# Trunk kernel, end of the last feed-forward layer: other chunk sizes, and the last 384 tokens multiplied with the weights moving

## The chip, the cores and the metric

The kernel runs on one core of one Trainium2 chip. The metric is the device time of one execution in microseconds (us): the median of the runs, 2497.24 us before the change (three runs, 2496.61 to 2497.68). One further execution was recorded by the profiler, and all views below are of that one.

The engines are named as in the profile: PE is the matrix engine (PEld its loads of the stationary operand), DVE the vector engine, ACT the scalar engine, POOL the GpSimd engine, SP the engine that issues most transfers.

## What is computed

Two layers over 640 tokens (512 of a new stream, 8 times 16 of running streams) of width 1024. A layer is a half-step feed-forward, a mixer (short convolution and chunk-band attention), and a second half-step feed-forward. A final normalization ends it:

```python
def _rmsnorm(x, g):
    xf = x.astype(jnp.float32)
    y = xf * lax.rsqrt(jnp.mean(xf * xf, axis=-1, keepdims=True) + EPS)
    return y.astype(x.dtype) * g

def _swiglu(h, w_gu, w_down):
    gu = h @ w_gu
    g, u = jnp.split(gu, 2, axis=-1)
    return (jax.nn.silu(g) * u) @ w_down
...
        xp = xp + 0.5 * _swiglu(_rmsnorm(xp, norm_ffn2[l]), w_ffn2_gu[l], w_ffn2_down[l])
...
    y_prompt = _rmsnorm(xp, norm_final)
    y_sample = _rmsnorm(xs, norm_final)
```

The hidden width of the feed-forward is 2816, which is 22 tiles of 128; the width 1024 is 8 tiles of 128. Everything is float32.

## The kernel before

**Layout.** The residual stream `x` lies in SBUF as eight tiles `x[0]` to `x[7]`, features on the 128 partitions and the 640 tokens along them. Every float32 product is made of three products of a faster format: an operand is split into a rounded part `hi` (ACT casts it, line 340 for weights, tile `whi`) and the rest `lo` (DVE subtracts, line 345, tile `wlo`), and `hi*hi`, `hi*lo` and `lo*hi` are added up in PSUM. Weights come as slabs of 128x1024 in the order of use, loaded by SP (tile `raw`, 512 KB each), and at most three split slabs exist at once (`bufs=3`).

**The four feed-forwards** are a0, b0 (layer 0) and a1, b1 (layer 1). The order of each is laid out by `ffn_order` from a list of chunk sizes, `FFNS`. Within a chunk the gate and up products of each of its hidden tiles are made (`gate_up`, one hidden tile j at a time), and the down products of the chunk before are spread between them.

- `gate_up` multiplies a 2x2 arrangement of blocks with seven block products in place of eight (the Strassen-Winograd scheme). Each block product is twelve matmuls of 320 columns: tiles `pa`, `pb`, `pc` in PSUM, line 435. The sums of weight blocks that it needs are made by DVE on the slabs (line 282); for the slabs that `LEAN` names, one of these sums is made by POOL instead, with two transfers of which the second adds to the first (`lend`, lines 267 and 268, tile `lent`).
- A chunk of four tiles that does not reach the end (`by_seven`) has its down products made the same way, in two units of seven block products each (`down_rows`, tiles `da`, `db`, `dc`, line 1110). Their results go into `x` partly by DVE (line 1137), partly through SBUF (`c1`, `c5`, `u2`) and a POOL transfer that adds in place (line 1132).
- Any other chunk has its down products made plainly (`product`, tile `pd`, line 411).

b1 has the chunks 3, 4, 4, 4, 4, 3: the first is done plainly, four by seven, and the last is handed to `Final`. In the stream this reads: gate-up of tiles 0 to 2, then tile 3 to 6 with a plain piece of the first chunk's down product behind each, and so on; at the end gate-up 19 and 20, a `down_rows` unit, gate-up 21, a `down_rows` unit, and the end. a1 and a0 have the chunks 4, 4, 4, 4, 4, 2; b0 has 4, 4, 4, 4, 6.

**The end, `Final`** (lines 1884 to 1969), works in the layout of `x`, features on the partitions. The tokens fall into two parts, 384 and 256 (`PARTS`). For each part and each of the eight feature tiles m, `product` makes nine matmuls (three hidden tiles, three products each; tile `pdf`, line 1938) with a block of weights stationary and the tokens moving; `take` adds half of that to `x[m]` (DVE, line 1943), squares it (ACT, line 1945) and adds the squares up over m (DVE, line 282, tile `fsum`). When a part is through, the sum over the features, which lies across partitions, is made by narrow matmuls against ones (tile `npsf`, line 519); ACT takes the root (line 1956), DVE the reciprocal (line 1961), a product with `fold` (line 529) and two matmuls (tile `nbcf`, line 538) spread the result over the partitions again, and `out` scales each `x[m]` by it and by the gain (DVE, line 1967) and sends it off (line 1969, SP and ACT queues). For the second part all of this follows the last matmul.

**Order.** PE, DVE and ACT run in the order in which the program is written here (`tc.manual_schedule`); for the middle of a feed-forward, from tile `free` on, only PE does. SP and POOL take their instructions as the planner places them. PSUM has eight banks of 512 float32 a partition; `layout` deals them out, in b1 four as two `acc` tiles and four as `att`.

Of the kernel before, what the change touches and what calls it, by code (L numbers as in the profile page):

```python
# [10 lines left out]
F32 = mybir.dt.float32  # L11
# [35 lines left out]
        "a1": ((4, 4, 4, 4, 4, 2), 0), "b1": ((3, 4, 4, 4, 4, 3), 0)}  # L47

PARTS = slice(0, 3 * P), slice(3 * P, T)
# [10 lines left out]
LEAN = {"a0": (1, 6), "b0": (1, 5), "a1": (1, 5)}  # L60
# [27 lines left out]
def ffn_order(name):  # L88


    chunks, plain = FFNS[name]
    out, held, j0 = [], [], 0
    for n in chunks:
        ms = list(range(KT)) if held else []
        step = max(2, -(-KT // n))
        for j in range(j0, j0 + n):
            out.append(("std" if j < plain else "gu", j))
            if ms and by_seven(name, held[0]):
                for _ in range((ROWS if n > 2 else (1, 1)).count(j - j0)):
# [6 lines left out]
        j0 += n  # L106

    return out + [("cut", None)] + [("down", [(m, held)]) for m in range(KT)]
# [24 lines left out]
def stages():  # L133
# [10 lines left out]
    def ffn(name):  # L144
        held = 0
        for what, a in ffn_order(name):
            if what == "gu":
                plain(held)
                held = 0
                out.append("gu")  # L150
            elif what == "std":
                held += 2 * KT
            elif what == "cut":
                plain(held)
                held = 0
            elif what == "rows":
                plain(held)
                held = 0
                out.append("gu")
            else:  # L160
                held += sum(len(js) for _, js in a)
        plain(held)
# [28 lines left out]
def trunk(ctx: ExitStack, tc: tile.TileContext, xin, wst, small, pbias, samplebias, kcache, vcache,  # L191
          yout, ko, vo, co):
# [654 lines left out]
    def gate_up(fp, n, ex, first, tails, put, j, pair, later, at):  # L847
# [122 lines left out]
        def tail(weights=True):  # L970
# [206 lines left out]
    def ffn(name, fp, ex, goff, after, end=False):  # L1177
# [57 lines left out]
        for what, a in ffn_order(name):  # L1235
# [6 lines left out]
            if what == "gu":  # L1242
# [11 lines left out]
                gate_up(fp, f"{name}_{a}", ex, a == plain, tails, act.__setitem__, a, pair, later,  # L1254
                        a - chunk_at(name, a)[0])
# [5 lines left out]
            js = a[0][1]  # L1261
# [622 lines left out]
    class Final:  # L1884


        def __init__(self):
            self.st = Stats("f")
            self.ssum = [pool[0].tile([P, c.stop - c.start], F32, tag=t, name=f"fsum{a}", bufs=1)
                         for a, (c, t) in enumerate(zip(PARTS, ("ssum", "rho")))]  # L1890

        def all(self, ops):
            ws = [[tiles.take() for _ in ops] for m in range(KT)]
            flush()
            rr = pool[0].tile([P, T], F32, tag="cap", name="frr", bufs=6)[:, PARTS[0]]
            A, B = PARTS

            for m in range(KT):
                self.product(0, m, ops, ws[m])
                self.take(0, m, m < KT - 1)  # L1900
            ends = self.ssum[0], self.sq
            for m in range(KT):
                self.product(1, m, ops, ws[m])
                if m == 1:
                    self.ps = att("npsf0")[:, : A.stop // P]
                    for b in range(A.stop // P):
                        self.st.column(self.ps[:, b : b + 1], ends, b)
                    self.root(0)
                if m == 4:
                    self.st.spread([att(f"nbcf0_{i}")[:, : A.stop // 2] for i in range(2)], self.ssum[0], rr)  # L1910
                if m == 5:
                    self.ps = acc("npsf1")[:, :, 0]
                    self.add(self.ssum[1], True)
                if m > 4:
                    self.add(self.sq)
                self.take(1, m, m < 4)
                if m == 2:
                    self.turn(0)
                for k in {5: (0,), 6: (1, 2)}.get(m, ()):
                    self.out(k, A, rr)  # L1920
            self.add(self.sq, False, True)
            self.root(1)
            for k in range(3, 6):
                self.out(k, A, rr)
            self.turn(1)
            for k in range(6, KT):
                self.out(k, A, rr)
            ps = acc("nbcf1")[:, :, : (B.stop - B.start) // 2]
            self.st.rows([ps[:, i] for i in range(2)], self.ssum[1])
            for k in range(KT):  # L1930
                self.out(k, B, ps)

        def product(self, a, m, ops, ws):
            n = PARTS[a].stop - PARTS[a].start
            self.pd = att(f"pdf{a}_{m}")[:, :n]
            for k, ((xh, xl), (wh, wl)) in enumerate(zip(ops, ws)):
                for j, (w, z) in enumerate(((wh, xh), (wh, xl), (wl, xh))):
                    PE.matmul(self.pd, w, z[:, PARTS[a]], start=k == 0 and j == 0,
                              stop=k == len(ops) - 1 and j == 2)

        def take(self, a, m, added):
            xm = x[m][:, PARTS[a]]
            DVE.scalar_tensor_tensor(out=xm, in0=self.pd, scalar=0.5, in1=xm, op0=ALU.mult, op1=ALU.add)
            self.sq = self.ssum[a] if m == 0 else tmp(f"sqf{a}_{m}")[:, : xm.shape[1]]
            ACT.activation(self.sq, xm, AF.Square)
            if m and added:
                add(self.ssum[a], self.ssum[a], self.sq)

        def add(self, z, start=False, stop=False):

            for b in range(2):
                self.st.column(self.ps[:, b : b + 1], [z], b, start, stop)

        def root(self, a):
            cs = slice(PARTS[a].start // P, PARTS[a].stop // P)
            ACT.activation(self.st.s[:, cs], self.ps, AF.Sqrt,
                           bias=epst[:, 0:1], scale=1.0 / D)

        def turn(self, a):
            cs = slice(PARTS[a].start // P, PARTS[a].stop // P)  # L1960
            DVE.reciprocal(self.st.r[:, cs], self.st.s[:, cs])
            self.st.turn(self.ssum[a], self.st.r[:, cs])

        def out(self, k, c, rr):
            z = x[k][:, c]
            y = z if c == PARTS[0] else halves(z)
            DVE.scalar_tensor_tensor(out=y, in0=y, scalar=sm[:, O_GF + k : O_GF + k + 1],
                                     in1=rr, op0=ALU.mult, op1=ALU.mult)
            (ACT if c == PARTS[1] and k % 2 else SP).dma_start(yout[:, k, c], x[k][:, c])
# [34 lines left out]
def _stream(i):  # L2004
# [9 lines left out]
    for l in range(L):  # L2014
        def ffn(name, gu, down):
# [3 lines left out]
            for what, a in ffn_order(name):  # L2019
# [11 lines left out]
                elif what == "rows":  # L2031
# [5 lines left out]
                                         for o in range(2) for m in ms[r::2]]))  # L2037
                else:
# [25 lines left out]
def _layout(inputs):  # L2064
# [21 lines left out]
    return {"xin": xin, "wst": _stream(i), "small": small, "pbias": pbias, "samplebias": sbias, "kcache": kc, "vcache": vc}  # L2086
# [3 lines left out]
    "yout": (P, KT, T),  # L2090
# [38 lines left out]
```

## Time and profile before

| what | us |
| --- | --- |
| median of three runs | 2497.24 |
| lowest, highest | 2496.61, 2497.68 |
| the profiled execution, its own time | 2496.82 |
| its span, first to last instruction | 2495.0 |
| busy PE, DVE, ACT, POOL in it | 2476.9, 2136.4, 1343.9, 281.9 |

The span and what lies around it differ by 1.82 us. Times in the views count from the start of the span. In the **chain of waits** a row is the start, the length and the work of one piece of the chain that ended last, with the number of instructions merged in it; its times for PE are those of the matmuls' ends. In the **timeline** a row is the start, the duration, engine, line, operation, output and inputs, shape and number of instructions; matmuls overlap, so their pace is read from start to start and not from the duration. In the **windows** a row is a stretch of time, its length, and the busy time of PE, PEld, DVE, ACT and POOL with the number of instructions, then the granted PE clock, the share of the DMA engines and GB/s. In the **groups** a row is line, engine, operation, tiles, shape and count, then busy us and mean ns of one, then the engine's idle time before them and what ended it.

### The profile page before, as it was taken

Reading aid. Unit: us, or ns where it says so; the run is one execution under the profiler, and the core shown is the slowest. Engines: PE = TensorE matmul, PEld = TensorE weight load, DVE = VectorE, ACT = ScalarE, POOL = GpSimd, SP = SyncE. Lnnn points to the kernel's source line nnn. Section 1 sums busy time; section 2 is a strip of 40 time slices with the busy share of each in tenths; the row PEclk is TensorE's granted clock in tenths of the full one; section 3 lists DMA queues with packets and bytes.
Section 4 is the critical chain, followed back from the end, with each engine's and each line's share of the span. In section 5 each row is a group of like instructions: output and inputs, shape, how many; then the busy total and the mean of one; then the engine's idle time right before and its main releaser. Section 6 shows DMA issues by size and latency. Waiting matters only on the chain.

```text
span 2495.0 us, 44032 instructions
## 1 busy us (share of the span) xinstructions
PE 2476.9 (99%) x17424; PEld 2426.2 (97%) x17424; DVE 2136.4 (86%) x3510; ACT 1343.9 (54%) x2122; POOL 281.9 (11%) x429
## 2 busy tenths in 40 slices
PE   8999999999999999999999999999999999999998
PEld 8999999889999999999999999998899999999998
DVE  7999998888777899998799999998886778899997
ACT  6555556665444555555665555566644455455553
POOL 0211112211000001011001111122110000011111
PEclk9999999999999999999999999999999999999999
DMA  4443444335223234445334443453342232243433
GB/s 154 127 118 100 123 117 127 108 111 168 77 89 109 90 101 109 108 117 121 98 102 111 108 116 106 104 127 119 120 157 85 77 98 81 85 110 108 123 102 101
DMA packets 107087, 275.18 MB, mean 110 GB/s; under 512 B 12128, under 2 KB 50656, under 8 KB 106880
## 3 DMA queue, kind: packets, MB, share of 16 engines
q1 hardware_dynamic: 69120, 219.71, 27.6%
q0 software_dynamic: 36896, 52.01, 11.2%
q8 instruction: 136, 2.23, 0.4%
q10 hardware_dynamic: 864, 0.65, 0.1%
q14 instruction: 71, 0.58, 0.1%
HBM read 228.47 MB, written 7.94 MB: 95 GB/s over the span
## 4 chain that ended last, share of the span: by engine, by line
PE 92%; DVE 4%; ACT 2%; issue 1%; DMA 1%; SPq 0%; DVEq 0%; ACTq 0%; POOLq 0%
PE pab L435 12%; PE paa L435 11%; PE pcb L435 6%; PE daa L1110 6%; PE pca L435 5%; PE dab L1110 4%; PE py L411 4%; PE po L411 4%; PE qa L435 4%; PE pbb L435 3%; PE dca L1110 3%; PE pba L435 3%; PE ma_cv L435 2%; PE ma_qk L435 2%; PE pv L1597 2%; PE dcb L1110 2%
## 5 line engine op out<-in xcount | busy, mean ns | idle before, releaser
L340 ACT CAST whi<-raw 128x1024 fp32r<-128x1024 f32 (+2 forms) x568 | 505.8, 894 | 389.7 <-PE pba L435 41.8
L345 DVE TENSOR_TENSOR wlo<-raw,whi 128x1024 fp32r<-128x1024 f32 (+2 forms) x568 | 580.3, 1024 | 153.9 <-ACT whi L340 150.6
L340 ACT CAST whi<-s 128x1024 fp32r<-128x1024 f32 (+1 forms) x156 | 148.6, 953 | 289.5 <-issue 107.9
L435 PE MATMUL pab<-xhib,whi 128*128 128x320 f32 x704 | 217.9, 309 | 0.0
L435 PE MATMUL pab<-xlob,whi 128*128 128x320 f32 x704 | 217.4, 309 | 0.0
L435 PE MATMUL pab<-xhib,wlo 128*128 128x320 f32 x704 | 217.3, 309 | 0.0
L435 PE MATMUL paa<-xloa,whi 128*128 128x320 f32 x640 | 197.7, 309 | 0.6 <-DVE xloa L672 0.6
L435 PE MATMUL paa<-xhia,whi 128*128 128x320 f32 x640 | 198.0, 309 | 0.2 <-DVE ga L282 0.2
L435 PE MATMUL paa<-xhia,wlo 128*128 128x320 f32 x640 | 197.7, 309 | 0.0
L345 DVE TENSOR_TENSOR wlo<-s,whi 128x1024 fp32r<-128x1024 f32 (+1 forms) x156 | 170.9, 1095 | 4.4 <-ACT whi L340 4.4
L1132 POOL DMA_DIRECT2D x<-c_b x64 | 56.6, 1026 | 841.9 <-DVE x L1137 502.4
L1132 POOL DMA_DIRECT2D x<-c_a x80 | 71.0, 1044 | 573.6 <-ACT ahia L1014 205.4
L435 PEld LDWEIGHTS pab<-xhib,whi 128*128 128x128 f32 x704 | 132.1, 188 | 1.1 <-issue 0.9
L435 PEld LDWEIGHTS pab<-xlob,whi 128*128 128x128 f32 x704 | 132.1, 188 | 0.0
L435 PEld LDWEIGHTS pab<-xhib,wlo 128*128 128x128 f32 x704 | 132.1, 188 | 0.0
L435 PEld LDWEIGHTS paa<-xhia,whi 128*128 128x128 f32 x640 | 120.1, 188 | 1.3 <-DVE ga L282 0.5
L435 PEld LDWEIGHTS paa<-xloa,whi 128*128 128x128 f32 x640 | 120.1, 188 | 1.1 <-DVE xloa L672 1.1
L435 PEld LDWEIGHTS paa<-xhia,wlo 128*128 128x128 f32 x640 | 120.1, 188 | 0.2
L435 PE MATMUL pcb<-xhib,wlo 128*128 128x320 f32 x352 | 108.9, 309 | 0.0
L435 PE MATMUL pcb<-xhib,whi 128*128 128x320 f32 x352 | 108.7, 309 | 0.0
L435 PE MATMUL pcb<-xlob,whi 128*128 128x320 f32 x352 | 108.7, 309 | 0.0
L282 DVE TENSOR_TENSOR raw<-s,raw 128x512 f32<-128x512 f32 x156 | 106.4, 682 | 0.0
(741 smaller groups left out, 8046.7 us busy)
## 6 DMA issues: line engine op xcount, KB each, us to landing
raw<-in_wst SPq DMA_DIRECT2D x376, 512.0 KB, 3.5
x<-c_a POOLq DMA_DIRECT2D x80, 160.0 KB, 4.4
x<-c_b POOLq DMA_DIRECT2D x64, 160.0 KB, 3.8
kc<-in_kcache SPq DMA_DIRECT2D x32, 256.0 KB, 4.7
vc<-in_vcache SPq DMA_DIRECT2D x16, 512.0 KB, 4.4
lent<-in_wst POOLq DMA_DIRECT2D x26, 256.0 KB, 4.0
x<-u_a POOLq DMA_DIRECT2D x40, 160.0 KB, 4.0
x<-u_b POOLq DMA_DIRECT2D x32, 160.0 KB, 4.2
```

Source lines behind the costliest of these rows:

```text
L282: DVE.tensor_tensor(out=out, in0=a, in1=b, op=op)
L340: ACT.copy(hi[:, d], src[:, c])
L345: DVE.tensor_tensor(out=lo, in0=src, in1=hi.bitcast(F32), op=ALU.subtract)
L411: PE.matmul(ps[:, a, :HT], w, x[a] if isinstance(x, tuple) else x[:, a * HT : (a + 1) * HT], start=first and j == 0 and not seeded, stop=l ...
L435: PE.matmul(ps, a, b, start=start and kp == 0 and j == 0, stop=stop and kp == NP - 1 and j == 2, skip_group_check=True)
L1110: PE.matmul(ps[u], w, y, start=start and i == 0 and j == 0, stop=i == 1 and j == 2, skip_group_check=True)
L1132: POOL.dma_start(x[ms[2 * u + r]][:, cols], z[:, u], accum_op=ALU.add)
L1597: PE.matmul(pv[t], xx[:, t * P : (t + 1) * P], w[:, kk * AW : (kk + 1) * AW], start=c == 0 and kk == 0 and j == 0, stop=c == KT // 2 - 1 a ...
```

## The change

The chunks of b1 become 4, 4, 4, 4, 4, 2 and `LEAN` gets an entry for b1. So five chunks are done by seven, the first among them, and two hidden tiles are left for the end; the last two `down_rows` units follow each other.

In the end the tokens fall into 256 (`FEAT`) and three groups of 128 (`GROUPS`). The 256 are done as before, with six matmuls a feature tile in place of nine. For each group of 128, `x` is turned by eight PE transposes into two PSUM banks (tokens on the partitions, 512 features each), and twelve matmuls add the down product to that, with the tokens' block stationary and 512 columns of weights moving. Each such half is squared by ACT with a running sum along the row; the row's sum gives the token's factor without a sum across partitions. The first half is multiplied by the gain at once (DVE) and by the factor later (ACT), the second half by both in one DVE instruction; each half goes out with a transfer of its own, one from SP and one from ACT. The gain comes as a new input of 128x1024, the same row on every partition, and these tokens leave through a new output `yrows`. The factor one half of the feed-forward is folded into the last two hidden tiles (`halve`). A root is taken of an unused value behind the first squares.

```diff
-        "a1": ((4, 4, 4, 4, 4, 2), 0), "b1": ((3, 4, 4, 4, 4, 3), 0)}
-
-PARTS = slice(0, 3 * P), slice(3 * P, T)
+        "a1": ((4, 4, 4, 4, 4, 2), 0), "b1": ((4, 4, 4, 4, 4, 2), 0)}
+
+FEAT = 2 * P
+GROUPS = (T - FEAT) // P
...
-LEAN = {"a0": (1, 6), "b0": (1, 5), "a1": (1, 5)}
+LEAN = {"a0": (1, 6), "b0": (1, 5), "a1": (1, 5), "b1": (1, 5)}
...
             else:
-                DVE.tensor_tensor(out=u, in0=u, in1=g, op=ALU.mult)
+                if halve:
+                    DVE.scalar_tensor_tensor(out=u, in0=u, scalar=0.5, in1=g, op0=ALU.mult, op1=ALU.mult)
+                else:
+                    DVE.tensor_tensor(out=u, in0=u, in1=g, op=ALU.mult)
...
+            self.ssum = pool[0].tile([P, FEAT], F32, tag="ssum", name="fsum", bufs=1)
+            self.acc = sp.tile([P, 2 * GROUPS], F32, tag="facc", name="facc", bufs=1)
+            self.root = sp.tile([P, 3 * GROUPS], F32, tag="froot", name="froot", bufs=1)
 
         def all(self, ops):
-            ws = [[tiles.take() for _ in ops] for m in range(KT)]
+            ws = [slab(hold[0])[0] for _ in ops]
             flush()
+            layout("e", 0)
+            self.g = wp.tile([P, D], F32, tag="raw", name="gfin", bufs=3)
+            SP.dma_start(self.g, gfin)
+            rr = pool[0].tile([P, T], F32, tag="cap", name="frr", bufs=6)[:, :FEAT]
+            st, nb = self.st, FEAT // P
+            self.rows = [[pr(f"prow{i}{h}") for h in range(2)] for i in range(2)]
+            self.y = [pool[0].tile([P, D], F32, tag="raw", name="yrow0", bufs=1)]
+            self.y += [wp.tile([P, D], F32, tag="raw", name=f"yrow{i}", bufs=3) for i in range(1, GROUPS)]
 
             for m in range(KT):
+                self.product(m, ops, ws)
+                self.take(m)
+                if m == 0:
+                    ACT.activation(early, self.ssum[:, 0:1], AF.Sqrt)
+            for i in range(2):
+                self.turned(i)
+            ps = att("npsf")[:, :nb]
+            for b in range(nb):
+                st.column(ps[:, b : b + 1], (self.ssum, self.sq), b)
+            ACT.activation(st.s[:, :nb], ps, AF.Sqrt, bias=epst[:, 0:1], scale=1.0 / D)
+            DVE.reciprocal(st.r[:, :nb], st.s[:, :nb])
+            st.turn(self.ssum, st.r[:, :nb])
+            self.half(0, 0, ops, ws)
+            self.half(0, 1, ops, ws)
+            st.spread([att(f"nbcf{i}")[:, : FEAT // 2] for i in range(2)], self.ssum, rr)
+            self.rows.append([att(f"prow2{h}") for h in range(2)])
+            self.turned(2)
+            for k in range(4):
+                self.out(k, rr)
+            self.half(1, 0, ops, ws)
+            for k in range(4, 6):
+                self.out(k, rr)
+            self.half(1, 1, ops, ws)
             for k in range(6, KT):
+                self.out(k, rr)
+            for h in range(2):
+                self.half(2, h, ops, ws)
+
+        def product(self, m, ops, ws):
+            self.pd = att(f"pdf{m}")[:, :FEAT]
             for k, ((xh, xl), (wh, wl)) in enumerate(zip(ops, ws)):
                 for j, (w, z) in enumerate(((wh, xh), (wh, xl), (wl, xh))):
+                    PE.matmul(self.pd, w[:, m * P : (m + 1) * P], z[:, :FEAT], start=k == 0 and j == 0,
                               stop=k == len(ops) - 1 and j == 2)
 
+        def take(self, m):
+            xm = x[m][:, :FEAT]
+            add(xm, self.pd, xm)
+            if m > 1:
+                add(self.ssum, self.ssum, self.sq)
+            self.sq = self.ssum if m == 0 else tmp(f"sqf{m}")[:, :FEAT]
             ACT.activation(self.sq, xm, AF.Square)
+
+        def turned(self, i):
+            c = slice(FEAT + i * P, FEAT + (i + 1) * P)
+            for m in range(KT):
+                h, o = divmod(m, KT // 2)
+                PE.matmul(self.rows[i][h][:, o * P : (o + 1) * P], x[m][:, c], ident, is_transpose=True,
+                          start=o == 0, stop=False, skip_group_check=True)
+
+        def half(self, i, h, ops, ws):
+            tokens = slice(FEAT + i * P, FEAT + (i + 1) * P)
+            c = slice(h * CH // 2, (h + 1) * CH // 2)
+            ps, y = self.rows[i][h], self.y[i]
+            for k, ((xh, xl), (wh, wl)) in enumerate(zip(ops, ws)):
+                for j, (z, w) in enumerate(((xh, wh), (xl, wh), (xh, wl))):
+                    PE.matmul(ps, z[:, tokens], w[:, c], start=False,
+                              stop=k == len(ops) - 1 and j == 2, skip_group_check=True)
+            s = self.acc[:, 2 * i + h :][:, 0:1]
+            part, root, r = (self.root[:, 3 * i + o :][:, 0:1] for o in range(3))
+            ACT.activation(tmp(f"sqr{i}{h}")[:, : CH // 2], ps, AF.Square, accum_out=s)
+            if h == 0:
+                DVE.tensor_tensor(out=y[:, c], in0=ps, in1=self.g[:, c], op=ALU.mult)
+                DVE.tensor_scalar(out=part, in0=s, scalar1=1.0 / D, scalar2=EPS, op0=ALU.mult, op1=ALU.add)
+                return
+            ACT.activation(root, s, AF.Sqrt, bias=part, scale=1.0 / D)
+            DVE.reciprocal(r, root)
+            DVE.scalar_tensor_tensor(out=y[:, c], in0=ps, scalar=r, in1=self.g[:, c],
+                                     op0=ALU.mult, op1=ALU.mult)
+            SP.dma_start(yrows[i][:, c], y[:, c])
+            c = slice(0, CH // 2)
+            ACT.activation(y[:, c], y[:, c], AF.Copy, scale=r)
+            ACT.dma_start(yrows[i][:, c], y[:, c])
+
+        def out(self, k, rr):
+            z = x[k][:, :FEAT]
+            DVE.scalar_tensor_tensor(out=z, in0=z, scalar=sm[:, O_GF + k : O_GF + k + 1],
                                      in1=rr, op0=ALU.mult, op1=ALU.mult)
+            SP.dma_start(yout[:, k], z)
```

`layout("e", 0)` deals the eight PSUM banks anew, four as `pr` and four as `att`.

More of the change, by code (lines that the diff above doesn't have):

```diff
@@ L159, in ffn @@
                 out.append("gu")
+            elif what == "ends":
+                held += KT * len(a)
             else:
@@ L2037, in ffn @@
                                          for o in range(2) for m in ms[r::2]]))
+                elif what == "ends":
+                    held += [d[m][j] for j in a for m in range(KT)]
                 else:
```

84 lines of the change are left out of this document (13 added, 71 removed).

## The prediction

> **What bounds the kernel now.** I read the page first, then the busy time by windows, then the chain of waits over the last feed-forward, then the timeline of each engine behind it.
>
> ```profile
> span 2495.0 us, 44032 instructions
> ...
> 2200.00:2300.00 100.00, 100.00 (x684) 100.00 (x683) 91.54 (x147) 52.33 (x74) 16.06 (x18) 1.00 0.46 115
> 2488.00:2495.00 7.00, 0.00 (x0) 0.00 (x0) 3.51 (x9) 0.00 (x0) 0.00 (x0) 0.50 0.64 225
> ```
>
> Inside b1 PE has no gap (100 of 100 us), with DVE close behind at 91.54. So there a matmul less is time less, as long as DVE keeps up. The last 7 us are the opposite: PE does nothing, DVE scales, the transfers land.
>
> ```profile
> 2459.14 0.35 PE pdf L1938 x2
> 2459.49 1.87 PE dab L1110 x12
> 2461.36 2.80 PE pdf L1938 x16
> ...
> 2488.77 2.74 DVE x L1967 x7
> ```
>
> In the chain the last `down_rows` unit would end at 2461.36 - 0.35 = 2461.01 without the two early `pdf` matmuls. From there to the end of the span are 33.99 us: this is what the new end replaces. I call the end of that unit T0 and work out first how far T0 moves, then how long the new end is.
>
> **Part 1: the chunks.** Four plain pieces of chunk 0 go, two `down_rows` units of seven block products come.
>
> ```profile
> 835.16 1.76 PE pab L435 x12
> ...
> 910.85 1.77 PE dab L1110 x12
> ...
> 1636.80 2.00 PE dba L1110 x12
> ...
> 1647.61 14.08 PE pda L411 x96
> ...
> 2068.24 1.76 PE pab L435 x12
> ...
> 2119.48 5.28 PE pdb L411 x36
> ```
>
> Removed: 4 x 5.28 = 21.12. Added: 2 x 7 x 1.76 = 24.64. That is 3.52 more on PE (the moved hidden tile leaves the end, below). Whether DVE can feed it is read from b0, which already begins with four by seven and the same `LEAN`: from 835.16 to its first `down_rows` at 910.85 are 75.69 us for six gate-ups of 7 x 1.76 = 12.32, so 1.77 over. b1 now: 2068.24 to 2119.48, 51.24 for four, 1.96 over. So the more costly preparation on DVE, ACT and POOL is hidden behind PE's block products there, and I cost it at nothing; without that cover it is the fourth rival. Two `down_rows` units in a row stand at the end of a1: its second unit's second block took 2.00 against 1.76, and the plain product behind it began with no gap. That is 0.24 more. T0 moves by 3.76, bounds 3.5 (no such gap, b0's 0.2 gained) and 4.2 (the gap twice, 0.2 for b0's way): to 2464.77.
>
> **Part 2: PE's work in the new end**, paces read from start to start in the timeline.
>
> ```profile
> 429.80 0.39 PE L1597 MATMUL pv<-whi,hhim 128*128 128x512 f32 x1
> ...
> 433.88 0.39 PE L1597 MATMUL pv<-whi,hhim 128*128 128x512 f32 x1
> ...
> 514.73 2.34 PE L1681 MATMUL ptp<-ident,s 128*128 128x128 f32 x20
> 516.83 0.39 PE L435 MATMUL ma_qk<-thi,whi 128*128 128x320 f32 x1
> ...
> 2473.34 0.28 PE L1938 MATMUL pdf<-ahib,whi 128*128 128x256 f32 x1
> ...
> 2475.36 0.28 PE L1938 MATMUL pdf<-ahib,wlo 128*128 128x256 f32 x1
> ...
> 2479.76 0.59 PE L538 MATMUL nbcf<-fsum,ones 64*128 64x192 f32 x4 [0.19 <-DVE fsum L529]
> ...
> 2481.55 0.31 PE L519 MATMUL npsf<-ones,fsum 128*32 128x1 f32 x16
> ...
> 2482.05 0.38 PE L1938 MATMUL pdf<-ahib,whi 128*128 128x256 f32 x1
> ```
>
> 256 tokens moving: 18 matmuls, 2.02 over 17 steps, 0.119 each; 48 of them are 5.7. Weights moving, 512 columns, token block stationary, is what the `pv` product of the mixer does: 19 matmuls, 4.08 over 18 steps, 0.227; a half of six is 1.36, six halves 8.2. Transposes: 20 in 2.10, 0.105 each; 24 are 2.5. Sums for two columns with two summands: 0.50. Spread: 0.59. Together 17.5. The six halves have six banks, so PE waits for no evacuation in between.
>
> A page of the Trainium skill speaks against the transposes: "TensorE: Matmul & The Clock Gate", section "Part 4: PE-mode transpose", gives about 275 ns for one. It is a rival below.
>
> **Part 3: what PE waits for in it.** Times from here are from T0.
>
> ```profile
> 1647.96 0.88 DVE L1137 SCALAR_TENSOR_TENSOR x<-daa,x 128x320 f32<-128x320 f32 x2
> ...
> 2460.60 2.43 POOL L1132 DMA_DIRECT2D x<-u_b  x2
> ...
> 2475.52 1.28 ACT L1956 ACT_TABLE_LOAD   x1
> 2476.81 0.26 ACT L1956 ACTIVATE nrmsf<-npsf,epst 128x3 f32<-128x3 f32 x1
> ...
> 2480.49 0.42 DVE L282 TENSOR_TENSOR fsum<-fsum,sqf 128x256 f32<-128x256 f32 x1 [0.54 <-ACT sqf L1945]
> 2480.84 0.42 DVE L1943 SCALAR_TENSOR_TENSOR x<-pdf,x 128x256 f32<-128x256 f32 x1
> ```
>
> In a1 DVE was done with the unit's last results at 1647.96 + 0.88, T0 + 1.23. A step over 256 columns takes it 0.42, the next starts 0.35 later. The first square (an estimate of 0.42 from the same width on DVE) ends near 2.1; then the root that stands behind it makes ACT load its table, 1.28, and takes 0.26: the second square ends near 4.0. Moved forward to here, the load holds up the squares queued behind it on ACT, and DVE with them, because the running sum waits for the square in DVE's own queue, ahead of the next feature tile. From 4.0 DVE needs 0.42 and five more tiles of 0.70: the last sum at about 7.9, the last square with it. PE, with four `att` banks, is not held in the products (tile 3's bank is free by 4.8, product 7 starts at 5.0); it ends them at 5.7, the sixteen transposes at 7.4, and waits until 8.0: **0.6 of stall**. The bounds are 0 (table load as early as it could be) and 2.0 (a step of 0.42 + 0.42 in place of 0.70 and 0.6 of hand-offs).
>
> A rule would make more of the load: the Trainium skill, "ScalarE: Activation LUTs", section "What ACT_TABLE_LOAD costs", puts a drain of about 1380 ns beside the 1283 ns. Here the root began at 2476.81, right where 2475.52 + 1.28 ends, so the trace shows no drain behind the load. By the rule the stall would be 2.0 and the forecast 2493.0.
>
> The transposes read tokens that POOL still adds into. Its last two additions were issued from 2460.60 to 2463.03, 0.4 before the old T0 and 2.0 after it. A landing 4.0 behind an issue (the `lent` row below, also from POOL; an estimate here) is at most T0 + 4.8 for the second's start; the transposes begin at 5.7. Hidden, 0.9 to spare; each us of lateness beyond costs one. The gain's load (512 KB, SP) is needed at 10 by the first multiplication, and its buffer is given up by the slabs before T0, with SP's queue empty of weights by then: hidden by about 10 us of PE work. If not, its landing is paid.
>
> **Part 4: after the last matmul.** On PE the sums end at 8.5, two halves at 11.3, the spread at 11.9, eight transposes at 12.7, four halves at 18.2.
>
> ```profile
> 456.34 1.87 ACT L1603 ACTIVATE v<-pv,ninvm 128x512 f32<-128x512 f32 x3
> ...
> 519.31 0.72 ACT L1844 ACTIVATE yc<-yc,st 128x512 f32<-128x512 f32 x1
> 519.92 0.19 ACT L1844 ACTIVATION_READ_ACCUMULATOR yc<-yc,st 128x1 f32 x1
> ...
> L1969 ACTq DMA_DIRECT2D out_yout<-x x4: 339/344/354, 2489.2 to 2491.5; - x4
> ...
> L1687 DVE COPY pt<-ptp 128x512 f32<-128x512 f32 x22 | 14.0, 680 | 3.1 <-PE ptp L1681 3.1
> ...
> 2488.30 3.22 DVE L1967 SCALAR_TENSOR_TENSOR x<-x,sm,nbcf 128x256 f32<-128x256 f32 x8
> ```
>
> ACT does for each pair of halves two squares with a running sum (0.61 and 0.09 each until the next can start, 0.70), a root 0.26, a scaled copy of 512 columns (1.87 / 3 = 0.62), the issue of a transfer 0.34, and waits some 0.3 for DVE's reciprocal in the middle: 2.9, against 2.72 of PE. So ACT falls behind a little, and the copies of `nbcf` come on top; I put the last square at 19.5 rather than 18.9, bounds 18.9 and 20.5. Then the root 0.26, the reciprocal and its hand-off 0.2, DVE's multiplication from PSUM 0.68 (the row of that width): 20.65. Now the last DVE step ends at 2491.52 and the span 3.5 later, with 128 KB in the last transfer; here two of 256 KB leave at once. The 7 us window moved 225 GB/s, so 384 KB more is at most 1.7; I take 0.5, bounds 0 and 1.7. The new end lasts 20.65 + 3.5 + 0.5 = **24.65**.
>
> **The sum.** 2464.77 + 24.65 = 2489.4 against a span of 2495.0: **5.6 less**. The profiled execution took 2496.82, 0.42 under the median of the runs; 2496.82 - 5.6 = 2491.2 for it, and 2497.24 - 5.6 = **2491.6** for the median. Read another way: 33.99 becomes 24.65, and 3.76 of that is given back as `down_rows`. With the cheap bounds (0.3 in part 1, 0.6, 0.6, 0.5) it is 2489.6; part 3, ACT and transfers at their dear bounds (0.4, 1.4, 1.0, 1.2) give 2495.6.
>
> **The rivals.**
>
> First, *ACT and DVE pace the end.* If nothing of ACT's steps overlaps, a pair costs 2 x (0.72 + 0.19) + 0.26 + 0.62 + 0.34 + 0.3 = 3.3, 0.4 more in each of the two pairs ahead of the last square; with the stall at 2.0 and the transfers 0.5 dearer the loss is 0.8 + 1.4 + 0.5 = 2.7: 2494.3. For it: three engines hand on in strict order, and DVE's eight `out` steps stand between reciprocals. Against it: ACT's own steps do overlap in the rows of part 4 (519.31 to 519.92 is 0.61 for a step of 0.72).
>
> Second, *transposes at their full duration.* A transpose's record is about 0.27 long, and if PE could not overlap them, 24 would cost 24 x (0.27 - 0.105) = 4.0 more: 2495.6. Twenty in 2.34 speak against it; that these are added onto by later matmuls is not in any row.
>
> Third, *the change doesn't do what it says:* by seven and turned, PE's work could be no less. The window from 2488 on shows PE empty, so its old end lies up to 27 behind T0; the new one lies at 18.2, and T0 itself 3.76 later. For no gain at all some 5 us of new waits are needed, and those are the first two rivals; it gets no chance of its own.
>
> Fourth, on the other side, *the lent slabs come late at the start of b1.*
>
> ```profile
> lent<-in_wst POOLq DMA_DIRECT2D x26, 256.0 KB, 4.0
> ...
> L340 ACT CAST whi<-lent 128x512 fp32r<-128x512 f32 x13 | 8.1, 620 | 2.1 <-DMA lent<-in_wst 0.7 <-PE pab L435 0.7 <-PE paa L435 0.7
> ```
>
> b1 has none now and gets four, each two transfers of 4.0 one after the other, on POOL. From the point where the second lands after ACT wants to cast, PE waits; if it is late by one transfer, four slabs cost 4 x 4.0 = 16: 2507.6, slower. Against it: thirteen lent slabs held ACT up by 0.7 in all.
>
> **Chances.** Forecast 0.66, first rival 0.15, second 0.09, fourth 0.10. What this kernel's measurement can tell from no change is about 0.2%, 5.0 us, so "faster" ends at 2492.2, only 0.6 above the forecast. Of the forecast's 0.66 I give 0.56 to below that and 0.10 to above, as its own bounds are lopsided upwards. Faster 0.56; within 0.2% 0.10 + 0.15 + 0.09 = 0.34; slower 0.10. The range reaches from just below the sum of the cheap bounds to 2498.0, beyond the dear ones and the first two rivals together with 2 us of unknown waits; it leaves the fourth rival out. The forecast's own range is 2489.6 to 2495.6.
>
> **What would show it.** In the changed kernel's chain: T0 near 2464.8 with no new PE idle between 2068 and there (else part 1 or the fourth rival); a gap of about 0.6 on PE ahead of `npsf` (part 3); `prow` matmuls 0.227 apart and transposes 0.105 apart (part 2, second rival); the last square starting within 0.6 of its last matmul (first rival); 5.2 or less from the start of the last root to the end (0.26 + 0.2 + 0.68 + 4.0). The prediction is wrong if T0 moves by over 4.2, if PE waits inside the six halves, or if the end behind the last matmul is longer than 7.5.

## The result, and the profile after

| | before | after |
| --- | --- | --- |
| median, 12 runs each on the same chip | 2497.06 | 2491.43 |
| lowest, highest | 2496.57, 2498.21 | 2491.31, 2492.54 |
| the profiled execution, its span | 2496.82, 2495.0 | 2491.9, 2490.1 |
| T0, the end of the last `down_rows` unit | 2461.01 | 2464.56 |
| from T0 to the end of the span | 33.99 | 25.54 |

Ratio 0.9978 (95% interval 0.997 to 0.9986, which is 3.5 to 7.5 us): 5.6 us less by the medians, against 5.6 predicted. The two profiled executions differ by 4.9, because the one of after was 0.5 above its own median and the one of before 0.2 below. T0 is read as before, from the start and duration of the last block product: 2464.25 + 0.31. Each part of the forecast can be checked by these two lengths: T0 moved by 3.55 (predicted 3.76), and the new end lasts 25.54 (predicted 24.65).

First the start of b1, where the first chunk is now made by seven. From the chain of waits of the changed kernel (start, length, work), and from its windows over the same stretch (start and end, length, busy PE, PEld, DVE, ACT, POOL, granted clock, DMA share, GB/s):

```profile
2105.12 3.52 PE pab L440 x24
...
2453.74 2.02 PE dbb L1118 x12
```
```profile
2068.00:2120.00 52.00, 52.00 (x389) 50.99 (x388) 48.27 (x78) 31.77 (x51) 2.85 (x4) 1.00 0.34 102
```

The chain stays on PE, a block product every 1.76 us, and PE is busy for all of the 52 us. What the new units ask for is there, but hidden: DVE has 48.27 us of work in this window and POOL 2.85, where the kernel before has 45.43 and 0 (its row is below, among the experiments). The second unit's second block took 2.02, as in a1.

Now the end. From the timeline of the changed kernel (start, duration, engine, line, operation, output and inputs, shape, count, and in brackets the engine's idle time before it and what ended it):

```profile
2464.25 0.31 PE L1118 MATMUL dab<-t4hib,wlo 128*128 128x320 f32 x1
...
2470.31 1.91 PE L1962 MATMUL prow<-ident,x 128*128 128x128 f32 x16
2472.25 0.24 PE L524 MATMUL npsf<-ones,fsum 128*32 128x1 f32 x8
...
2472.70 0.24 PE L524 MATMUL npsf<-ones,sqf 128*32 128x1 f32 x8 [0.21 <-ACT sqf L1955]
...
2473.00 0.50 PE L1972 MATMUL prow<-whi,ahib 128*128 128x512 f32 x1
...
2482.56 0.39 PE L1972 MATMUL prow<-wlo,ahib 128*128 128x512 f32 x1
...
2466.60 1.28 ACT L1917 ACT_TABLE_LOAD   x1
2467.89 0.20 ACT L1917 ACTIVATE early<-fsum 128x1 f32<-128x1 f32 x1
...
2478.56 0.43 ACT L551 COPY frr<-nbcf 128x128 f32<-128x128 f32 x2 [0.46 <-ACT yrow L1987]
...
2479.03 1.67 DVE L1992 SCALAR_TENSOR_TENSOR x<-x,sm,frr 128x256 f32<-128x256 f32 x4 [0.90 <-ACT frr L551]
...
2481.45 0.29 ACT L1981 ACTIVATE froot<-facc,froot 128x1 f32<-128x1 f32 x1 [0.50 <-DVE froot L1979]
...
2482.26 0.72 ACT L1987 ACTIVATE yrow<-yrow,froot 128x512 f32<-128x512 f32 x1 [0.51 <-DVE froot L1982]
...
2483.01 0.38 ACTq L1988 DMA_DIRECT2D out_yrows<-yrow  x1
2483.43 0.60 ACT L1976 ACTIVATE sqr<-prow 128x512 f32<-128x512 f32 x1 [0.45 <-ACT yrow L1987]
...
2484.02 0.59 ACT L1976 ACTIVATE sqr<-prow 128x512 f32<-128x512 f32 x1
2484.50 0.20 ACT L1976 ACTIVATION_READ_ACCUMULATOR sqr<-prow 128x1 f32 x1
2485.00 0.29 ACT L1981 ACTIVATE froot<-facc,froot 128x1 f32<-128x1 f32 x1 [0.30 <-DVE froot L1979]
```

Against the steps of the forecast, from T0: the first half begins at 8.44 (predicted 8.5), the last matmul ends at 2482.56 + 0.39, T0 + 18.39 (18.2), the last square with its sum at 2484.70, T0 + 20.14 (19.5), and from the start of the last root to the end of the span are 5.1 (at most 5.2). PE nearly kept the forecast. The last square ended 0.64 later than forecast, of which 0.19 was PE's, and another 0.3 went by ahead of the root, which waited for DVE's small step of L1979. It began 1.07 behind the last matmul (2484.02 less 2482.95).

### The profile page after: what moved, and what is told of

It is laid out like the page before. It is cut to its first block, busy times and chain, and to the rows that moved or that the text cites. A ratio compares the mean times of both kernels' runs of the same rounds, so it can differ in the third digit from the quotient of the medians.

```text
span 2490.1 us, 43907 instructions
## 1 busy us (share of the span) xinstructions
PE 2475.0 (99%) x17312; PEld 2422.6 (97%) x17312; DVE 2140.2 (86%) x3532; ACT 1355.9 (54%) x2151; POOL 294.9 (12%) x449
## 4 chain that ended last, share of the span: by engine, by line
PE 93%; DVE 4%; ACT 2%; issue 1%; DMA 0%; ACTq 0%; SPq 0%; DVEq 0%; POOLq 0%
PE pab L440 12%; PE paa L440 11%; PE pcb L440 6%; PE daa L1118 6%; PE pca L440 5%; PE dab L1118 5%; PE py L416 4%; PE po L416 4%; PE qa L440 4%; PE pbb L440 3%; PE dca L1118 3%; PE pba L440 3%; PE dcb L1118 2%; PE ma_cv L440 2%; PE ma_qk L440 2%; PE pv L1605 2%
## 5 line engine op out<-in xcount | busy, mean ns | idle before, releaser
L350 DVE TENSOR_TENSOR wlo<-raw,whi 128x1024 fp32r<-128x1024 f32 (+1 forms) x569 | 580.3, 1022 | 156.1 <-ACT whi L345 152.9
L345 ACT CAST whi<-raw 128x1024 fp32r<-128x1024 f32 (+1 forms) x569 | 505.1, 891 | 381.7 <-PE pbb L440 47.2
L1140 POOL DMA_DIRECT2D x<-c_b x72 | 62.7, 1001 | 582.9 <-ACT ahib L1022 205.8
```

The lines of the kernel that those rows point to most:

```text
L345: ACT.copy(hi[:, d], src[:, c])
L350: DVE.tensor_tensor(out=lo, in0=src, in1=hi.bitcast(F32), op=ALU.subtract)
L1140: POOL.dma_start(x[ms[2 * u + r]][:, cols], z[:, u], accum_op=ALU.add)
```

## The experiments

Each further kernel was timed in five rounds beside the kernel before, on three chips in all; the first row has the lowest and the highest median of the kernel before on them. In the following, "start of b1" is the start of its first `pab` matmul. It differs by up to 1 us between profiled executions with the same code ahead of it, so T0 is compared relative to it: 2461.01 - 2068.08 = 392.93 before, 2464.56 - 2067.99 = 396.57 after. Where the code ahead of T0 is the same, that length agrees within 0.05 (396.55 to 396.60 in the table), so the two lengths tell small differences better than the medians, though each comes from one execution. Medians under 0.5 us apart are not told apart by their runs: those without the early root (2490.41 to 2491.28) and those with three edits (2490.09 to 2491.04) overlap.

| kernel | median | ratio (95% interval) | start of b1 to T0 | T0 to end |
| --- | --- | --- | --- | --- |
| before | 2496.8 to 2497.1 | | 392.93 | 33.99 |
| after | 2491.43 | 0.9978 (0.997 to 0.9986) | 396.57 | 25.54 |
| the chunks alone | 2498.77 | 1.0007 (0.9998 to 1.0016) | 396.60 | 31.79 |
| the end alone | 2494.66 | 0.9991 (0.9982 to 0.9999) | 393.27 | 32.10 |
| after without `LEAN` for b1 | 2492.99 | 0.9984 (0.9975 to 0.9993) | 398.37 | 25.24 |
| early root ahead of the products | 2492.81 | 0.9982 (0.9974 to 0.9991) | 398.54 | 24.98 |
| no early root | 2490.63 | 0.9974 (0.9964 to 0.9984) | 396.56 | 25.07 |
| spread first | 2491.0 | 0.9976 (0.9966 to 0.9986) | 396.57 | 25.32 |
| both, and bias first | 2490.26 | 0.9973 (0.9963 to 0.9983) | 396.58 | 24.43 |
| one hidden tile in the end | 2498.25 | 1.0004 (0.9995 to 1.0013) | 407.3 | 21.7 |
| transfers issued by SP | 2489.73 | 0.9971 (0.9961 to 0.9982) | 396.59 | 23.91 |
| a scaled copy later | 2489.75 | 0.9972 (0.9961 to 0.9983) | 396.55 | 23.85 |

### The two halves of the change

The chunks alone: the kernel before, with

```diff
-        "a1": ((4, 4, 4, 4, 4, 2), 0), "b1": ((3, 4, 4, 4, 4, 3), 0)}
+        "a1": ((4, 4, 4, 4, 4, 2), 0), "b1": ((4, 4, 4, 4, 4, 2), 0)}
-LEAN = {"a0": (1, 6), "b0": (1, 5), "a1": (1, 5)}
+LEAN = {"a0": (1, 6), "b0": (1, 5), "a1": (1, 5), "b1": (1, 5)}
```

> The kernel before with only the chunks of b1 and its LEAN entry changed; the old end (384 and 256 tokens, features on the partitions) then multiplies two hidden tiles in place of three. Theory (the two parts are separate gains): the end of the last down_rows unit moves 3.5 later as in the changed kernel; the old end loses 24 matmuls of 384 columns (4.2) and 24 of 256 (2.9), of which only some 1.5 is kept because the root, its spreading and DVE stay as long: 2494.9, range 2493.5 to 2495.5. Rival (turning alone makes the gain, the chunks only cost): the old end keeps its length on DVE and ACT, 2497.1 + 3.5 = 2500.6.

The end alone: the changed kernel with these two lines as they were before.

> The changed kernel with the chunks and LEAN of before; the new end multiplies three hidden tiles. Theory: the end of the last down_rows unit stays at 2461.0; the new end is longer by 2.3 (its products by 2.9, without the wait of 0.6 ahead of the sums) and by six times 0.68, 4.1, and shorter by some 0.7 since ACT and DVE keep up with slower halves: 25.5 + 5.7 = 31.2 against 34.0, so 2494.3, range 2493.8 to 2495.2. Rival (the new end pays only together with fewer hidden tiles): 2497.1.

The chunks alone cost 1.7 us, the end alone gained 2.4, and the two together 5.6, 4.9 more than the sum. The 1.7 is not told from no change by its interval, but it lies outside the theory's range, which ended at 2495.5, and short of the rival's 2500.6; the end alone lies in its theory's range. T0 moves by 3.67 for the chunks, where 3.5 was expected. For the end alone it moves by 0.34: the kernel before does two matmuls of its end in that time (0.35), and its T0 leaves them out. What differs is how long the end behind T0 is. From the windows of the kernel before and of the chunks alone:

```profile
2068.00:2120.00 52.00, 52.00 (x387) 50.79 (x386) 45.43 (x70) 29.24 (x44) 0.00 (x0) 1.00 0.27 86
...
2473.00:2483.00 10.00, 9.81 (x149) 9.07 (x149) 5.54 (x14) 5.32 (x12) 0.00 (x0) 1.00 0.01 2
```
```profile
2473.00:2483.00 10.00, 6.72 (x84) 5.79 (x82) 5.44 (x15) 5.00 (x11) 0.00 (x0) 0.83 0.00 1
```

From 2473 to 2483 PE was 9.81 us busy in the old end with three hidden tiles, and 6.72 with two: PE is idle for a third of it, and the end has become only 2.2 us shorter (33.99 to 31.79), where the expected 2494.9 needed some 5.7. Why, the timeline of the chunks alone tells, and below it the chain of waits of the kernel before:

```profile
2465.68 0.33 PE L1938 MATMUL pdf<-alob,whi 128*128 128x384 f32 x1
2465.86 0.33 PE L1938 MATMUL pdf<-ahib,wlo 128*128 128x384 f32 x1
...
2470.05 0.53 ACT L1945 ACTIVATE sqf<-x 128x384 f32<-128x384 f32 x1 [1.09 <-DVE x L1943]
2471.67 0.52 ACT L1945 ACTIVATE sqf<-x 128x384 f32<-128x384 f32 x1 [1.09 <-DVE x L1943]
```
```profile
2465.80 0.56 DVE x L1943
...
2467.42 0.56 DVE x L1943
```

Six matmuls of a feature tile take PE 6 x 0.173 = 1.04 us, nine took 1.56. The old end's `take` goes from DVE (the addition) to ACT (the square) and back to DVE (the sum, which stands ahead of the next addition in DVE's queue), and needs 1.62 a tile in both kernels, whatever PE does. With three hidden tiles the two paces are nearly equal, so a tile less for PE gives next to nothing there. In the new end `take` puts the sum behind the next addition. There PE sets the pace: in the version without the early root (further below) it is busy for all of the 17.90 us from T0 to the last matmul, and the chain of waits runs through it up to the first squares:

```profile
2463.83 5.92 PE pdf L1944 x48
...
2471.86 2.98 PE prow L1970 x12
```

The windows behind T0, of the end alone and, as a sum from 2464.4 on, of the changed kernel:

```profile
2460.50:2492.60 32.10, 25.21 (x187) 21.70 (x185) 16.25 (x40) 13.45 (x32) 1.68 (x2) 0.98 0.36 103
```
```profile
sum 25.70, PE 18.31 PEld 15.64 DVE 14.86 ACT 12.29 POOL 1.56; mean PE 6.10 PEld 5.21 DVE 4.95 ACT 4.10 POOL 0.52
```

A hidden tile less is 6.9 us less of PE, and the end falls by 6.56 (32.10 to 25.54). That the two are so close is a balance of two other terms. With three hidden tiles PE also waits 0.29 and 0.76 for the split of its third slab:

```profile
2462.75 0.39 PE L1946 MATMUL pdf<-ahib,wlo 128*128 128x256 f32 x1 [0.76 <-DVE wlo L350]
```

Behind the last matmul, on the other hand, the end alone lasts 5.85 and the changed kernel 7.15. So the new chunks are worth nothing without the new end, and the new end little without the new chunks. No run has the old end with the new order of `take` and nothing else, so how much of the gain is that order and how much the turned tokens stays open.

The row of the chunks alone also shows a granted PE clock of 0.83 against 1.00. In windows of 2 us it was 0.58 and 0.56 from 2478 to 2482, after PE had been busy for 1.28 of the 4 us before, and `pdf` matmuls of 256 columns started 0.21 apart there and not 0.12. The chain of waits runs through DVE and ACT in that stretch, so what the lower clock cost is not shown. The chunks alone also ran 1.1 above their profiled execution by the median. The mean clocks of their eleven runs are 0.996 to 0.998, lowest in the longest run, against 0.998 and 0.999 in the kernel before beside them; what makes them vary stays open.

### What `LEAN` is worth

The changed kernel with `LEAN` as before.

> The changed kernel without the LEAN entry of b1: DVE makes the four sums that POOL makes now. Theory (DVE has slack enough in the first chunks, PE sets the time there): 2491.4, within 0.5. Rival (POOL's sums are what lets DVE keep up): four sums of 0.68 each late, 2494.1.

1.6 us slower than the changed kernel, between the two expectations; the slack that the theory gave DVE was not there. The chain of waits at the start of b1, without `LEAN`:

```profile
2088.97 1.77 PE pab L440 x10
...
2090.83 0.50 DVE gb L287
...
2097.95 0.62 ACT whi L345
...
2109.52 1.15 DVE wlo L350
...
2110.71 1.73 PE pab L440 x10
```

From 2090.7 to 2110.7 the chain runs through DVE and ACT, which prepare the slabs, and no longer through PE, as it did in the same stretch of the changed kernel above. T0 comes 1.80 later (398.37 against 396.57). With four additions of weight blocks on POOL, DVE stays just ahead.

### The wait ahead of the sums

The early root, which makes ACT load its table between the first and the second square, was first moved ahead of the products and given a constant:

```diff
+            ACT.activation(early, epst, AF.Sqrt)
             for m in range(KT):
                 self.product(m, ops, ws)
                 self.take(m)
-                if m == 0:
-                    ACT.activation(early, self.ssum[:, 0:1], AF.Sqrt)
```

> The changed kernel with the early root, and so the load of ACT's table, placed ahead of the eight products of the end, where ACT has nothing to do, in place of behind the first square. Theory (the load delays the squares and with them the sums, PE waits some 0.5 for them, and everything behind is shifted by it): 2490.9 and no gap ahead of the sums. Rival (ACT and DVE pace the six halves whenever these start): 2491.4, unchanged. A drain of 1.4 behind the load, as a rule has it, would show as a free stretch of ACT behind the load.

The run missed both, and for a reason outside the end: the root waits for nothing late, and it was run at the start of b1, where it added two table loads, its own and the one that loads the former table again. ACT's copies for PE came later by that. From the timeline of that kernel, and its window over the start of b1:

```profile
2082.08 1.28 ACT L1913 ACT_TABLE_LOAD   x1
...
2084.53 1.28 ACT L971 ACT_TABLE_LOAD   x1
...
2473.19 1.28 ACT L1922 ACT_TABLE_LOAD   x1
```
```profile
2068.00:2120.00 52.00, 50.30 (x375) 49.03 (x374) 46.43 (x75) 32.97 (x52) 2.86 (x4) 1.00 0.35 102
```

PE stood idle for 1.70 of the 52 us, and T0 came 1.97 later. Behind T0 the run does answer: with the load back at the root of the sums (L1922, where PE is busy with the first half) the end took 24.98 instead of 25.54. The clean form is to leave the early root out:

```diff
-                if m == 0:
-                    ACT.activation(early, self.ssum[:, 0:1], AF.Sqrt)
```

> The changed kernel without the early root on the running sum (its table load stood between the first and the second square). Theory (that load made the 0.5 us wait ahead of npsf): the wait at npsf falls from 0.5 to about 0.1, the load now stands at the root of the six groups and lies behind the first half (1.36 us of PE), T0 stays at 2464.6, the end lasts 25.0 instead of 25.5 us, the time is 2490.9. Rival (the wait at npsf comes from DVE's pace over the eight tiles): the wait stays at 0.5 and the time at 2491.4; if the load now holds up the spread, PE waits up to 0.7 us ahead of nbcf.

End 25.07 (25.0 expected), T0 unmoved, 2490.63 us: the theory holds. From the timeline of that kernel:

```profile
2471.42 0.24 PE L524 MATMUL npsf<-ones,fsum 128*32 128x1 f32 x8
2471.51 0.22 PE L524 MATMUL npsf<-ones,sqf 128*32 128x1 f32 x8
...
2470.74 1.28 ACT L1921 ACT_TABLE_LOAD   x1
2472.03 0.26 ACT L1921 ACTIVATE nrmsf<-npsf,epst 128x2 f32<-128x2 f32 x1
```

The two `npsf` groups start 0.09 apart, where the changed kernel has 0.45. The load begins before its root's input is there, runs beside PE, and the root follows with 0.01 between.

### What holds up the last squares

The halves' twelve matmuls were separated from their evacuation, so that the spread's matmuls and ACT's copies of `nbcf` come between the two for the second half:

```diff
-            self.half(0, 1, ops, ws)
+            self.mm(0, 1, ops, ws)
             st.spread([att(f"nbcf{i}")[:, : FEAT // 2] for i in range(2)], self.ssum, rr)
+            self.post(0, 1)
```

> The changed kernel with the spread's matmuls and ScalarE copies put between the second half's matmuls and its squares, roots and scaled copies; the early root stays. Theory (ACT fell behind because the copies of nbcf stood behind the first scaled copy, DVE's out steps started late and the reciprocals queued behind them): the copies begin near 2476.4 instead of 2478.6, the last square starts within 0.4 us of its last matmul instead of 1.07, the end is 0.7 shorter, the time 2490.7. Rival (ACT's own work of 2.9 us a pair is the pace, however it is ordered): the last square stays 1 us late, the time 2491.4.

A third of it came: the copies begin at 2475.93, the last square starts 0.77 behind its last matmul (0.4 expected), the end is 0.2 shorter (25.32), the time 2491.0, between theory and rival. Next, both edits together, with the bias of the root made ahead of the multiplication:

```diff
             if h == 0:
-                DVE.tensor_tensor(out=y[:, c], in0=ps, in1=self.g[:, c], op=ALU.mult)
                 DVE.tensor_scalar(out=part, in0=s, scalar1=1.0 / D, scalar2=EPS, op0=ALU.mult, op1=ALU.add)
+                DVE.tensor_tensor(out=y[:, c], in0=ps, in1=self.g[:, c], op=ALU.mult)
```

> Both of the edits before together, and the small step that makes the root's bias put ahead of DVE's multiplication of the first 512 features. Theory: 0.5 + 0.7 + up to 0.3 us less than the changed kernel, 2489.9 to 2490.2. Rival: the three waits hide each other and it is 2490.9.

2490.26, just above the theory's range; the end is 24.43. Its timeline shows what is left, 0.77 between the last matmul's end (2481.87) and the last square:

```profile
2480.88 0.72 ACT L1993 ACTIVATE yrow<-yrow,froot 128x512 f32<-128x512 f32 x1 [0.68 <-DVE froot L1988]
2481.63 0.38 ACTq L1994 DMA_DIRECT2D out_yrows<-yrow  x1
2482.05 0.60 ACT L1982 ACTIVATE sqr<-prow 128x512 f32<-128x512 f32 x1 [0.45 <-PE prow L1974]
...
2482.64 0.59 ACT L1982 ACTIVATE sqr<-prow 128x512 f32<-128x512 f32 x1
```

ACT waits 0.68 for DVE's reciprocal, then is held for 0.38 and more by issuing a transfer, while the first half of the last group has been ready since about 2480.5 (2481.87 less the 1.36 of the half behind it). Two further runs take away one each, the second on top of the first:

```diff
-            ACT.dma_start(yrows[i][:, c], y[:, c])
+            (ACT if i == GROUPS - 1 else SP).dma_start(yrows[i][:, c], y[:, c])
```

> The version with the three edits together (2490.26 us), and the transfers of the first two scaled halves issued from SP's queue instead of ACT's. Theory (ACT is still the late engine at the last pair, 0.77 us behind the last matmul, and 0.38 of that is the issue of a transfer): the last square starts 0.4 earlier, the end lasts 24.0 instead of 24.4 us, the time is 2489.85. Rival (the issue is not what ACT waits behind; DVE's reciprocal is, 0.68 late): the squares move by under 0.1 and the time stays at 2490.2.

```diff
-            for h in range(2):
-                self.half(2, h, ops, ws)
+            self.half(2, 0, ops, ws)
+            self.scaled(1)
+            self.half(2, 1, ops, ws)
```

> As the run before, and the scaled copy of the second group behind the first square of the third, so that ACT does not stand waiting for the second reciprocal while that half is ready. Theory: the last square starts within 0.3 us of the end of its last matmul, the end lasts 23.7 to 24.0 us, the time is 2489.6 to 2489.9. Rival (what follows, DVE's last multiplication or the last two transfers, takes the time back): no less than the run before.

The first gave what was expected: end 23.91, 2489.73 us. The second brought the square to where it was meant to be, but there was little left to gain: with the first, the square already started 0.21 behind its last matmul. The end is 0.06 shorter (23.85). The time, 2489.75, fits the theory's range and the rival alike, so it does not decide between them. From the timeline:

```profile
2481.66 0.39 PE L1975 MATMUL prow<-wlo,ahib 128*128 128x512 f32 x1
...
2482.08 0.60 ACT L1983 ACTIVATE sqr<-prow 128x512 f32<-128x512 f32 x1
...
2481.72 0.87 DVE L2004 SCALAR_TENSOR_TENSOR x<-x,sm,frr 128x256 f32<-128x256 f32 x2
...
2482.57 0.68 DVE L1986 TENSOR_TENSOR yrow<-prow,gfin 128x512 f32<-128x512 f32 x1
2483.17 0.15 DVE L1989 RECIPROCAL froot<-froot 128x1 f32<-128x1 f32 x1
2483.43 0.75 DVE L1990 SCALAR_TENSOR_TENSOR yrow<-prow,froot,gfin 128x512 f32<-128x512 f32 x1
```

The last square starts 0.03 behind its last matmul, but now DVE goes from step to step from 2481.72 to the reciprocal: two `out` steps, then the multiplication of the first half, then the reciprocal. The chain of waits runs through DVE here, though ACT's root, at 2483.09, ended only 0.08 before the reciprocal began; DVE's order alone would give little more. Both versions beat the kernel before and the changed one; 7.1 us under the kernel before on their chip.

### One hidden tile less in the end

The version with three edits, with the chunks 4, 4, 4, 4, 5, 1.

> As the run before, with the last FFN in chunks 4, 4, 4, 4, 5, 1: one hidden tile less in the end, seven block products more before it. Theory (each hidden tile costs the turned end 24 x 0.119 + 18 x 0.227 = 6.9 us of PE and down_rows 7 x 0.25 x 1.76 x 2 = 3.5 to 4 us, but the sums are paced by DVE and ACT at 8 us and the halves by ACT at 2.9 a pair, so that the end falls by 4 to 5 us only): 2489 to 2490. Rival (the end stays PE's): 2487. If five tiles in the fifth chunk break the preparation's pace: over 2492.

2498.25 us. A chunk of five is not done by seven here: its down product went the plain way, and the chain of waits shows it as one piece ahead of the end:

```profile
2440.30 35.21 PE pdb L416 x240
```

So T0 came 10.7 later. By seven, the expectation's own product (7 x 0.25 x 1.76 x 2) would have been 6.2 and not 3.5 to 4, so that against the 2.7 below, by estimate, the tile would have lost time even then. What the run answers is the end: 21.7 instead of 24.43. A hidden tile less took 6.55 us of PE's busy time out of it (17.89 to 11.34) and only 2.7 us of time, less than the 4 to 5 expected. ACT and DVE set this end: the last square began at 2491.42, 3.5 us after the last matmul, where it was 0.77 with two hidden tiles. This suggests that at two hidden tiles PE and the others are nearly even.

## Why the prediction was right

**T0: right.** 3.76 was forecast, and it was 3.55 as it stands, 3.64 relative to the start of b1. (The lower bound of 3.5 comes to 3.3 from the two terms that it names.) That the costlier preparation costs nothing held for the change as a whole (PE 52.00 of 52.00), but the cover is thin: the run without `LEAN` shows 1.80 without it. The prediction named PE's block products as the cover; it is these together with POOL's four additions.

**Late lent slabs, the slower rival: refuted.** PE has no idle time at the start of b1, nor up to T0 (64.40 busy of 64.40 us from 2400 on).

**PE's work: right.** 17.5 predicted; the last matmul ends 18.39 behind T0, and without the early root 17.90, with PE busy throughout. So the work was 0.4 dearer and the stall below cheaper than forecast. Transposes come 16 in 1.91, 0.109 apart at a duration of 0.273, and matmuls added onto them start without a gap, so the second rival falls. The Trainium skill, "TensorE: Matmul & The Clock Gate", "Part 4: PE-mode transpose", gives about 275 ns for one in a kernel: that is the duration here, and the forecast by the row held.

**The stall: right, cause shown.** 0.6 predicted. Between the two groups of `npsf` are 0.45, and 0.09 in the run without the early root, whose end is 0.47 shorter. The drain of about 1380 ns that the Trainium skill, "ScalarE: Activation LUTs", "What ACT_TABLE_LOAD costs", puts beside the load is not there: the root began at 2467.89, where 2466.60 + 1.28 ends, the load right behind the first square, and the stall of 2.0 that would follow did not come.

**Behind the last matmul: right in mechanism, too small.** The term "ACT falls behind a little", last square at 19.5, measured 20.14, and the root another 0.3 later. ACT's own pace was not the cause: the steps of a pair come to 3.0 from start to start, against 2.9 worked out. But ACT stood waiting for DVE's small steps (0.50 ahead of the second root, 0.51 ahead of its scaled copy), which were queued behind `out` steps, and issued transfers while a half was ready. This is the first rival in kind, at about a third of its price: the last square began 1.07 behind its last matmul, beyond the 0.6 that the prediction had set as the sign. Four edits of order, the early root among them, make the end 1.6 us shorter (25.54 to 23.91).

**The sum: closer than its parts.** T0 moved 0.2 less than forecast and the end took 0.9 more, so the profiled pair differs by 4.9 and not 5.6. That the medians agree with the forecast to 0.1 is luck. The parts are not additive, which the forecast did not say and did not need, because it costed the new end with two tiles as a whole. The estimate that failed is the one for the chunks alone, 2494.9: it took the old end for one that PE sets, and the old end was at the point where DVE and ACT set it.

## What to carry to other kernels

Before taking work off an engine, ask whether another engine's hand-offs run at nearly the same pace in that stage: here 1.56 us of PE stood beside 1.62 of DVE and ACT, and removing a third of PE's work alone was worth less than it cost (2.2 off the end, 3.67 more ahead of it). A change of order that frees the chain (a sum one step later, a queue with nothing urgent behind a wait) can make such a saving count. And in an end of a few microseconds, look in each engine's queue for what stands ahead of the one instruction that is waited for: bulk steps ahead of a reciprocal, a table load ahead of a square, a transfer's issue ahead of the last evacuation.

## What was not expected of the hardware

DVE's multiplication of a first half from PSUM began in no profile before ACT's square of the same half had ended, though both only read it. From the timeline of the changed kernel:

```profile
2475.25 0.19 ACT L1976 ACTIVATION_READ_ACCUMULATOR sqr<-prow 128x1 f32 x1
...
2475.47 0.69 DVE L1978 TENSOR_TENSOR yrow<-prow,gfin 128x512 f32<-128x512 f32 x1 [1.45 <-ACT sqr L1976]
```

DVE stood idle for 1.45 us and began right behind the read of ACT's sum. The profile takes what ended a wait from semaphore events, and names ACT's square here, so by the view a semaphore of the program orders the two. Whether the chip would need it was not tried.

Issuing one transfer of 256 KB from ACT holds its queue for 0.38 us and the next instruction began 0.42 behind the issue's start, about two thirds of a square of 512 columns (0.60); moving two of them to SP took 0.5 us off the end.
